# Two plain tiles of an up-projection as one sequence in a fixed order

## The chip, the core and the metric

The kernel runs on one core of a Trainium2 chip. The metric is device time in microseconds (us) of one execution of the whole program; lower is better. TensorE (PE) does the matrix products, VectorE (DVE), ScalarE (ACT) and GpSimd (POOL) work on tiles, SyncE (SP) issues the DMAs. Each of these engines has a queue of its own, and semaphores order the work between them.

## The reference, cut to what matters

One layer of a hybrid backbone: a mixer sub-layer, then a gated MLP with a 3x3 depthwise convolution on the token grid. There are 1024 tokens, 1024 channels, 2816 hidden channels (22 tiles of 128). The change lies where the MLP begins:

```
x   = x + mx[2] * ox                       # ox ends in the product with w_out
hx2 = modulate(rmsnorm(x, norm_ffn_w), mx[3], mx[4])
u, v = split(hx2 @ w_up, 2)                # 22 tiles of u, 22 tiles of v
u   = dwconv2d(u, conv_w, conv_b, 16, 64)  # 9 taps
h   = gelu(u) * v
x   = x + mx[5] * (h @ w_down)
```

Everything is float32. A float32 product is made of three products of a rounded part ("hi") and a remainder ("lo"): hi*hi, hi*lo, lo*hi. So each weight tile and each activation tile is split once: ACT writes hi (a copy to the rounded type), then DVE or POOL writes lo = x - hi.

## The kernel before

**Stages.** After the mixer, `wout` (L1108) makes the w_out product twice, once for each half of the tokens (512 each), 8 tiles of 24 matmuls each time, and adds the result to the residual tiles M0 to M7. Beside the second half, `norm` (L1093) normalizes the first half of the tokens, so that the eight blocks of the first half ("11" and "12", four each, in tiles A0 to A7) are ready when `wout` ends. The second half is normalized only when `wout` has ended, and that runs beside the first two tiles of the up-projection.

**Norm of a half.** `norm` adds up squares over partitions with matmuls against ones (L199), makes 1/sqrt of it in a chain of seven small operations (L182 to L188), spreads it over partitions with matmuls against a scaled identity (L208, L209), and then calls `apply1` for k = 0 to 7: DVE multiplies (a SCALAR_TENSOR_TENSOR, L157), ACT writes the hi half (h), ACT adds the shift in place (q), DVE writes the remainder l = q - h (TENSOR_TENSOR, L160). Blocks k = 0 to 3 are "t12", k = 4 to 7 are "s4"; they stand in tiles H0 to H3 and H8 to H11, and q in H12 to H15.

**Plain tiles.** `up_plain` (L1135) makes hidden tiles f = 0 and f = 1 in the plain way: u and v, for two halves of the tokens, 24 matmuls for each of the eight products (here u0, v0, u1, v1, each with "h0" and "h1" for the halves). u goes to a PSUM tile of pool psD (name d, 2 buffers), v to two of pool psS (name s, 4 buffers). When u is complete, `conv2d` (L1159) lets ACT write bias and middle tap (facc<-d,vec), and DVE adds eight taps (facc<-d,vec,facc); then ACT makes the GELU, DVE multiplies with v, and a DMA stores the tile.

**Strassen tiles.** From f = 2 on, `ups` (L1268) makes each tile with seven products ("11", "12", "s2", "s1", "s3", "s4", "22") of 12 matmuls. They need sums of the activation blocks: `blocks` (L1423) makes "s2", "s1" and "s3" for k = 0 to 3 from the normalized halves, mostly on POOL, and `blocks_late` makes "22" on DVE. In each k, POOL writes t1 (ssq<-H,A), DVE t2 = b22 - t1 (ssq<-H,ssq), ACT and DVE the two parts of t2, POOL t3 (sql<-H), and ACT and POOL the parts of t1 and t3. Product "s2" may begin when ACT has copied "11" out of PSUM (sql<-d), "s1" when DVE has added "12" (d<-d,sql) and ACT has copied "s2" (ssq<-d); these are the waits that `after` (L1250) sets.

**Order.** Up to `ups` a scheduler orders the instructions: `weave` mixes generators, and the scheduler moves instructions that are ready earlier ahead, on each engine apart. `ups` sets `self.pinned`, and from there what goes through `pin` (L1128) stays in the order in which the program writes it. Weights go through `wload` (L78): one DMA to a room raw (2 buffers), then the split into whi0/wlo0 or whi1/wlo1, in turn.

Of the kernel before, what the change touches and what calls it, by code (L numbers as in the profile page):

```python
# [45 lines left out]
class Builder:  # L46
# [129 lines left out]
    def rsqrt(self, pool, ps, n, inv, tag):  # L176

        nc = self.nc
        v = self.t(pool, n, tag + "v")
        a = self.t(pool, n, tag + "a")  # L180
        r = self.t(pool, n, tag + "r")
        nc.vector.tensor_scalar(v, ps, inv, EPS, op0=ALU.mult, op1=ALU.add)  # L182
        self.act(a, v, AF.Sqrt)
        nc.vector.reciprocal(r, a)
        self.tt(a, r, r)
        self.tt(a, a, v)
        nc.vector.tensor_scalar(a, a, -0.5, 1.5, op0=ALU.mult, op1=ALU.add)
        self.tt(r, r, a)  # L188
        return r

    def token_rs(self, pool, parts, n, inv, tag, ps=None):
# [9 lines left out]
        return self.rsqrt(pool, ps[:, :nch], nch, inv, tag)

    def spread(self, pool, r, out, tag):

# [930 lines left out]
    def up_plain(self, f, x, split):  # L1135

        pu = self.t(self.psD, T, "d")
        pv = [self.t(self.psS, H, "s") for _ in range(2)]
        wu = self.wload(self.A["wup"][f])
        wv = self.wload(self.A["wup"][NF + f]) if split else None  # L1140
        for n, hf in ((0, 0), (1, 0), (0, 1), (1, 1)) if split else ((0, 0), (0, 1), (1, 0), (1, 1)):
            if n and wv is None:
                wv = self.wload(self.A["wup"][NF + f])
            blocks = lambda: [x["b"][q][k] for q in (("11", "12"), ("t12", "s4"))[hf] for k in range(4)]
            while any(q is None for q in blocks()):
                next(x["blocks"])
            xh, xl = zip(*blocks())
            yield from self.gdense(pv[hf] if n else pu[:, hf * H : hf * H + H], wv if n else wu, xh, xl, [(0, H)])
            if (n, hf) == (0, 1):
                for _ in self.conv2d(f, pu):  # L1150
                    pass
                acc = self.convacc
        self.act(acc, acc, AF.Gelu_apprx_tanh)
        for i in range(2):
            self.tt(acc[:, i * H : i * H + H], acc[:, i * H : i * H + H], pv[i])
        self.st.dma_start(self.h_d[f], acc)
        yield
# [418 lines left out]
```

## Time and profile before

| | us |
|---|---|
| median of 3 runs | 2314.39 |
| lowest and highest of the runs | 2313.72, 2317.71 |
| profiled execution, its own time | 2316.08 |
| its span, first to last instruction | 2314.3 |
| PE busy in it | 2238.8 (97%) |
| plain tiles, from the first matmul to the first of the Strassen tiles | 1599.34 to 1651.68 |

The profiled execution is 1.69 us above the median, and 1.8 us of it lie outside its span. All places below are in us from the start of the span. A mean granted clock of 0.986 belongs to this execution; 1.00 is the full 2.4 GHz of TensorE, 0.50 is 1.2 GHz.

### The profile page before, as it was taken

What the parts mean: (1) busy time and instruction counts of PE and PEld (TensorE: products, weight loads), DVE (VectorE), ACT (ScalarE), POOL (GpSimd) and SP (SyncE); (2) the same over time, 40 slices, a digit from 0 to 9 for tenths busy, and PEclk for the clock granted to TensorE, in tenths of its full rate; (3) what the DMA queues carried; (4) which work ended last, traced back from release to release, by engine and by line L of the source; (5) the groups of instructions that cost most, each with busy time, mean ns of one, the idle gap of its engine ahead of it and who ended that gap; (6) DMA issues with size and microseconds to landing.
All of it is one profiled execution on the core that took longest, in us unless ns stands there. A gap on an engine that the chain in (4) does not pass through costs nothing.

```text
span 2314.3 us, 29745 instructions
## 1 busy us (share of the span) xinstructions
PE 2238.8 (97%) x11290; PEld 1852.4 (80%) x11290; DVE 1640.5 (71%) x2617; ACT 1150.1 (50%) x1781; POOL 330.0 (14%) x254
## 2 busy tenths in 40 slices
PE   6999999999999999999999999999889999999998
PEld 3778878778888888888888878888668888878888
DVE  4887877789978858767875675547877777774335
ACT  4577667667666647646635332334434444442121
POOL 0000000000000000000000000000757777740000
PEclk7999999999999999999999999999999999999999
DMA  6322322145335333524427775542022222244212
GB/s 250 96 69 73 95 83 65 62 126 159 122 107 172 114 121 106 159 85 130 155 90 267 234 231 191 171 139 73 28 73 82 83 82 82 80 161 129 77 55 73
DMA packets 87795, 274.88 MB, mean 119 GB/s; under 512 B 10434, under 2 KB 16610, under 8 KB 82404
## 3 DMA queue, kind: packets, MB, share of 16 engines
q1 hardware_dynamic: 87648, 272.97, 36.9%
q8 instruction: 89, 1.46, 0.3%
q14 instruction: 54, 0.44, 0.1%
q10 hardware_dynamic: 4, 0.01, 0.0%
HBM read 233.86 MB, written 39.08 MB: 118 GB/s over the span
## 4 chain that ended last, share of the span: by engine, by line
PE 76%; DVE 13%; DMA 5%; ACT 3%; issue 2%; POOL 1%; SPq 0%; POOLq 0%; DVEq 0%; ACTq 0%
PE d L125 30%; PE s L125 18%; PE d L1220 11%; PE s L1220 5%; PE s L986 2%; DMA adar<-in_ada 2%; PE s L651 2%; ACT L L163 1%; DVE wlo L160 1%; PE s L978 1%; DVE L L160 1%; DMA gk<-gd 1%; PE s L927 1%; PE s L926 1%; DVE facc L157 1%
## 5 line engine op out<-in xcount | busy, mean ns | idle before, releaser
L125 PE MATMUL d<-H,whi 128*128 128x512 f32 x2496 | 700.8, 398 | 1.8 <-DVE H L160 1.0
L125 PEld LDWEIGHTS d<-H,whi 128*128 128x128 f32 x2496 | 457.0, 188 | 97.1 <-issue 6.0
L125 PE MATMUL d<-H,wlo 128*128 128x512 f32 x1248 | 392.8, 393 | 1.8 <-DVE wlo L160 1.8
L163 ACT ACTIVATE whi<-raw 128x1024 fp32r<-128x1024 f32 (+2 forms) x194 | 185.7, 959 | 270.7 <-PE s L125 115.4
L125 PEld LDWEIGHTS d<-H,wlo 128*128 128x128 f32 x1248 | 232.9, 188 | 51.6 <-DVE wlo L160 3.5
L157 DVE SCALAR_TENSOR_TENSOR facc<-d,vec,facc 128x945 f32<-128x945 f32 (+2 forms) x176 | 214.6, 1221 | 72.9 <-ACT facc L163 68.6
L160 DVE TENSOR_TENSOR wlo<-raw,whi 128x1024 fp32r<-128x1024 f32 (+1 forms) x154 | 187.5, 1220 | 81.2 <-ACT whi L163 74.4
L125 PE MATMUL s<-H,whi 128*128 128x512 f32 x672 | 202.6, 390 | 1.9 <-ACT whi L163 1.9
L163 ACT ACT_TABLE_LOAD x102 | 130.9, 1283 | 85.9 <-DVE cacc L157 28.7
L1133 POOL TENSOR_TENSOR ssq<-H,A 128x512 f32<-128x512 f32 x4 | 6.0, 1493 | 1162.8 <-ACT H L163 1158.6
L125 PEld LDWEIGHTS s<-H,whi 128*128 128x128 f32 x672 | 125.8, 188 | 29.2 <-ACT whi L163 2.8
L125 PE MATMUL s<-A,whi 128*128 128x512 f32 x480 | 138.2, 390 | 1.0 <-POOL A L1133 1.0
L157 DVE SCALAR_TENSOR_TENSOR M<-s,mods,M 128x512 f32<-128x512 f32 (+1 forms) x72 | 49.5, 690 | 120.4 <-PE s L125 120.3
L125 PE MATMUL s<-H,wlo 128*128 128x512 f32 x336 | 126.0, 391 | 2.1 <-DVE wlo L160 2.0
L125 PEld LDWEIGHTS s<-A,whi 128*128 128x128 f32 x480 | 90.1, 188 | 20.1 <-POOL A L1133 1.4
L157 DVE SCALAR_TENSOR_TENSOR E<-E,cst 128x128 f32<-128x128 f32 x256 | 81.3, 344 | 20.5 <-ACT E L163 20.5
L163 ACT ACTIVATE m<-GU,dtt 128x128 f32<-128x128 f32 x256 | 78.7, 389 | 34.5 <-PE s L978 29.3
L157 DVE SCALAR_TENSOR_TENSOR m<-GL,dtt,m 128x128 f32<-128x128 f32 x256 | 77.7, 346 | 20.3 <-ACT m L163 20.1
L1220 PE MATMUL d<-A,whi 128*128 128x512 f32 x372 | 91.3, 395 | 0.0
L1220 PE MATMUL d<-A,wlo 128*128 128x512 f32 x348 | 85.9, 397 | 5.2 <-ACT ssq L163 5.2
L163 ACT ACTIVATE E<-E,cst 128x128 f32<-128x128 f32 x256 | 80.4, 389 | 17.5 <-DMA E<-csd 17.4
L125 PE MATMUL s<-A,wlo 128*128 128x512 f32 x240 | 83.1, 390 | 0.8 <-DVE wlo L160 0.8
(337 smaller groups left out, 4288.2 us busy)
## 6 DMA issues: line engine op xcount, KB each, us to landing
raw<-in_w SPq DMA_DIRECT2D x92, 512.0 KB, 3.6
E<-csd SPq DMA_DIRECT2D x32, 1024.0 KB, 7.1
A<-in_wup SPq DMA_DIRECT2D x40, 512.0 KB, 4.1
R<-csd SPq DMA_DIRECT2D x64, 256.0 KB, 4.7
adar<-in_ada SPq DMA_DIRECT2D x32, 512.0 KB, 4.0
hd<-facc SPq DMA_DIRECT2D x22, 512.0 KB, 5.1
gated<-sg SPq DMA_DIRECT2D x32, 256.0 KB, 3.8
gd<-y SPq DMA_DIRECT2D x32, 256.0 KB, 2.4
```

The costliest lines, as they stand in the source:

```text
L125: nc.tensor.matmul(o, a[:, k, :], b[k][:, xo + s : xo + e], start=(k == 0 and i == 0), stop=(k == kn - 1 and i == 2))
L157: self.pin(self.nc.vector.scalar_tensor_tensor(out, in0, s, in1, op0=op0, op1=op1))
L160: return self.pin(self.nc.vector.tensor_tensor(out, a, b, op=op))
L163: return self.pin(self.nc.scalar.activation(out, in_, f, **kw))
L651: nc.tensor.matmul(pg, a[:, q, :], b[:, s:e], start=(i == 0), stop=(i == 2))
L926: nc.tensor.matmul(ps[:, s - s2, 0, :], btok[:, s, :], xw[:, 0, s, :], start=True, stop=True)
L927: nc.tensor.matmul(ps[:, s - s2, 1, :], btok[:, 7 - s, :], xw[:, 1, 7 - s, :], start=True, stop=True)
L978: nc.tensor.matmul(psy[q, c, :], self.xt[:, c0 + c, q], m[:, h, c, :], start=True, stop=True)
L986: nc.tensor.matmul(pso[:, c, :], S[:, cc if d == 0 else 7 - cc, d, :], CT[:, cc * P : (cc + 1) * P], start=True, stop=True)
L1133: self.pin(self.nc.gpsimd.tensor_tensor(out, a, b, op=op))
L1220: q = self.pin(self.nc.tensor.matmul(ps, a[:, k, :], b, start=(k == 0 and i == 0 and p in ("11", "12", "s3")), stop=(k == 3 and i == 2), s ...
```

## The change

`up_plain` is replaced by `plain`, which writes both tiles out as one sequence of 64 steps (i = 0 to 63, three matmuls each) and sets `self.pinned` from its beginning. The eight products stand in the order u0 h0, v0 h0, u1 h0, u0 h1, v0 h1, u1 h1, v1 h1, v1 h0. At fixed steps it draws the next piece of the norm, of `blocks` ("sums"), of the two convolutions, and it loads and splits the weights of the first two Strassen products (their splits stood at the head of `ups`). The norm's small operations are pinned too, its PSUM rooms come from pool psS, and its waits are 3 and 4 steps where they were 5 and 3. The weights of u1 go to tiles A14 and A15; the raw weights of f = 3, which had these rooms, are loaded later. `self.wslot = 1` gives u0 the rooms whi0/wlo0 and v0 the rooms whi1/wlo1.

```diff
-        r = self.token_rs(p1, parts, n, 1.0 / D, "fr", self.t(self.psD, T, "d"))
+        room = lambda: self.t(self.psD, T, "d") if pool is None else self.t(pool, H, "s")
+        r = self.token_rs(p1, parts, n, 1.0 / D, "fr", room())
...
+    def plain(self, x, norm, sums):
+        C, b = self.CLASSIC, x["b"]
+        self.wslot = 1
+        w = {"u0": self.wload(self.A["wup"][0]), "v0": self.wload(self.A["wup"][NF])}
+        self.pinned = True
...
+        i = -1
+        for name, f, hf in (("u", 0, 0), ("v", 0, 0), ("u", 1, 0), ("u", 0, 1), ("v", 0, 1), ("u", 1, 1), ("v", 1, 1), ("v", 1, 0)):
...
+            for k in range(8):
+                i += 1
+                if i < 18:
+                    next(norm, None)
+                elif i % 2 == 0:
+                    next(sums, None)
+                for c in (0, 1):
+                    if i == 32 + 16 * c:
+                        conv[c] = [None, self.conv2d(c, pu[c])]
+                    if i in range(32 + 16 * c, 40 + 16 * c, 2):
+                        next(conv[c][1], None)
+                        conv[c][0] = conv[c][0] or self.convacc
+                    if i == 41 + 22 * c:
+                        next(conv[c][1], None)
+                        self.act(conv[c][0], conv[c][0], AF.Gelu_apprx_tanh)
+                if i == 33:
+                    w["v1"] = self.wload(self.A["wup"][NF + 1])
+                if i == 45:
+                    gate(0)
...
+                if i == 56:
+                    self.pslot = 1
+                    for p in ("11", "12"):
+                        self.up_split(C, p, x)
+                p = (("11", "12"), ("t12", "s4"))[hf][k // 4]
+                while b[p][k % 4] is None:
+                    next(norm)
+                bh, bl = b[p][k % 4]
+                for j, (m, n) in enumerate(((hi, bh), (hi, bl), (lo, bh))):
+                    self.pin(self.nc.tensor.matmul(ps, m[:, k, :], n, start=(k == 0 and j == 0), stop=(k == 7 and j == 2)))
+        for _ in sums:
+            pass
+        gate(1)
...
-            x["blocks"] = self.chain(self.norm(sums[1], H, apply1, self.WAIT), blocks())
-            self.weave(self.chain(*[self.up_plain(f, x, f == 0) for f in range(C)]), x["blocks"], self.RATIO[4])
+            for i in range(2):
+                self.up_load(C, i, x)
+            self.plain(x, self.norm(sums[1], H, apply1, (3, 4), self.psS), blocks())
```

**On DVE, the norm of the second half.** M are the residual tiles of k = 0, 1, ...; each H<-M is the multiplication of `apply1`, each H<-H,H the remainder l of a block. Before:

```order
L157 SCALAR_TENSOR_TENSOR H_1823_13111<-M_1685_12373,sc_7_81,d_13095 128x512
L157 SCALAR_TENSOR_TENSOR H_1825_13120<-M_1686_12374,sc_7_81,d_13095 128x512
L157 SCALAR_TENSOR_TENSOR H_1827_13129<-M_1687_12375,sc_7_81,d_13095 128x512
L157 SCALAR_TENSOR_TENSOR H_1829_13138<-M_1688_12376,sc_7_81,d_13095 128x512
L160 TENSOR_TENSOR H_1824_13113<-H_1823_13111,H_1824_13113 128x512
```

and after the change:

```order
L157 SCALAR_TENSOR_TENSOR H_1823_13106<-M_1685_12373,sc_7_81,s_13089 128x512
L160 TENSOR_TENSOR H_1824_13108<-H_1823_13106,H_1824_13108 128x512
L157 SCALAR_TENSOR_TENSOR H_1825_13115<-M_1686_12374,sc_7_81,s_13089 128x512
L160 TENSOR_TENSOR H_1826_13117<-H_1825_13115,H_1826_13117 128x512
L157 SCALAR_TENSOR_TENSOR H_1827_13124<-M_1687_12375,sc_7_81,s_13089 128x512
```

Four multiplications stood ahead of the first remainder; now each remainder stands right behind its own multiplication.

**On ACT, from the blocks' parts to the first copies of the Strassen tiles.** H and A<-ssq and <-sql are parts of the blocks, whi<-raw 128x1024 is the split of a weight tile of v1, facc<-d is the beginning of a convolution, facc<-facc a GELU, sql<-d the copy of product "11". Before (the two splits of 128x1024 are the weights of u1 and of v1):

```order
L163 ACTIVATE A_1845_13212<-ssq_13200 128x512
L163 ACTIVATE whi_1864_13300<-raw_13298 128x1024
L163 ACTIVATE H_1844_13205<-ssq_13201 128x512
L163 ACTIVATE H_1846_13218<-sql_13202 128x512
L163 ACTIVATE A_1851_13236<-ssq_13224 128x512
L163 ACTIVATE whi_1868_13364<-raw_13362 128x1024
L163 ACTIVATE facc_13239<-d_13034,vec_72 128x1024
L163 ACTIVATE H_1850_13229<-ssq_13225 128x512
```

and in the changed kernel, from the parts of k = 2 on:

```order
L163 ACTIVATE H_1851_13252<-ssq_13248 128x512
L163 ACTIVATE A_1853_13263<-ssq_13247 128x512
L163 ACTIVATE facc_13266<-d_13048,vec_72 128x1024
L163 ACTIVATE whi_1856_13275<-raw_13273 128x1024
L163 ACTIVATE H_1858_13282<-sql_13249 128x512
```

The beginning of the first convolution and the split of v1 stand behind the part H<-ssq of k = 2, which waits for DVE's t2 of k = 2; before, they stood ahead of it.

**On ACT, the GELU of tile 1 and the copy of "11".** facc_13352 and facc_13353 are the accumulators of tile 1; whi_1871 and wlo_1872 split the weights of "11" and "12". Before:

```order
L163 ACTIVATE facc_13352<-d_13295,vec_72 128x1024
L163 ACTIVATE wlo_1872_13426<-A_1801_13026 128x512
L163 ACT_TABLE_LOAD
L163 ACTIVATE facc_13239<-facc_13239 128x1024
L163 ACTIVATE whi_1873_13429<-raw_13420 128x512
L163 ACTIVATE wlo_1874_13433<-raw_13420 128x512
L163 ACTIVATE sql_13450<-d_13437 128x512
L163 ACTIVATE whi_1878_13454<-raw_13420 128x512
L163 ACTIVATE facc_13352<-facc_13352 128x1024
```

and after the change:

```order
L163 ACT_TABLE_LOAD
L163 ACTIVATE facc_13266<-facc_13266 128x1024
L163 ACTIVATE facc_13353<-d_13174,vec_72 128x1024
L163 ACTIVATE whi_1871_13395<-A_1801_13026 128x512
L163 ACTIVATE wlo_1872_13398<-A_1801_13026 128x512
L163 ACTIVATE facc_13353<-facc_13353 128x1024
L163 ACTIVATE whi_1873_13429<-raw_13377 128x512
L163 ACTIVATE wlo_1874_13433<-raw_13377 128x512
L163 ACTIVATE sql_13450<-d_13437 128x512
```

The second convolution begins behind the first GELU, and the copy of "11" stands behind the second GELU; before, it was the other way round in both.

## Rows read from the trace of the kernel before

**Rows 1.** Stretches: length, busy us of each engine, granted clock, DMA share, GB/s.

```profile
1599.30:1651.70 52.40, 49.05 (x218) 39.46 (x216) 41.20 (x49) 23.81 (x37) 30.22 (x20) 0.97 0.04 11
1651.70:1670.00 18.30, 13.10 (x48) 10.36 (x48) 16.38 (x15) 7.42 (x11) 12.16 (x9) 0.82 0.23 87
1670.00:1690.00 20.00, 16.75 (x71) 12.83 (x70) 18.45 (x16) 7.66 (x13) 11.82 (x8) 1.00 0.18 52
1690.00:1710.00 20.00, 14.90 (x53) 11.72 (x54) 10.82 (x13) 5.82 (x9) 9.27 (x7) 0.74 0.18 54
1710.00:1730.00 20.00, 20.00 (x90) 16.57 (x89) 14.34 (x15) 9.00 (x14) 14.60 (x12) 1.00 0.26 79
```

**Rows 2.** Timeline of PE: start, us, line, what; in brackets idle time and releaser.

```profile
1599.34 0.61 PE L125 MATMUL d<-A,whi 128*128 128x512 f32 x2
...
1603.42 0.28 PE L199 MATMUL d<-ones,ssq 128*128 128x1 f32 x2
...
1617.94 0.50 PE L125 MATMUL d<-H,whi 128*128 128x512 f32 x1 [1.01 <-DVE H L160]
...
1628.62 0.50 PE L125 MATMUL d<-A,wlo 128*128 128x512 f32 x1 [2.21 <-DVE wlo L160]
...
1651.68 2.95 PE L1220 MATMUL d<-A,whi 128*128 128x512 f32 x12
...
1665.27 5.23 PE L1220 MATMUL d<-A,wlo 128*128 128x512 f32 x12 [5.20 <-ACT ssq L163]
```

**Rows 3.** Timeline of ACT: hi splits of the first two up-projection weights.

```profile
1593.87 1.06 ACT L163 ACTIVATE whi<-raw 128x1024 fp32r<-128x1024 f32 x1 [3.73 <-PE s L125]
...
1599.31 1.06 ACT L163 ACTIVATE whi<-raw 128x1024 fp32r<-128x1024 f32 x1 [3.73 <-PE s L125]
```

**Rows 4.** Timeline of DVE: a weight's lo split, and the second half's norm.

```profile
1600.93 1.22 DVE L160 TENSOR_TENSOR wlo<-raw,whi 128x1024 fp32r<-128x1024 f32 x1
...
1608.81 2.72 DVE L157 SCALAR_TENSOR_TENSOR H<-M,sc,d 128x512 f32<-128x512 f32 x4 [0.58 <-PE d L209]
...
1618.41 0.74 DVE L157 SCALAR_TENSOR_TENSOR H<-M,sc,d 128x512 f32<-128x512 f32 x1
...
1621.48 0.68 DVE L160 TENSOR_TENSOR H<-H,H 128x512 fp32r<-128x512 f32 x1
```

**Rows 5.** Timeline of ACT: the hi half of the norm's last block.

```profile
1619.18 0.73 ACT L163 ACTIVATE H<-H,mods 128x512 fp32r<-128x512 f32 x1 [0.76 <-DVE H L157]
```

**Rows 6.** Timelines of POOL and DVE: operations of the blocks, beside each other.

```profile
1624.52 1.28 POOL L1133 TENSOR_TENSOR H<-sql,H 128x512 fp32r<-128x512 f32 x1
...
1624.59 1.76 DVE L160 TENSOR_TENSOR ssq<-H,ssq 128x512 f32<-128x512 f32 x1 [2.43 <-POOL A L1133]
...
1627.44 2.26 POOL L1133 TENSOR_TENSOR sql<-H 128x512 f32<-128x512 f32 x1
```

**Rows 7.** Timeline of DVE: taps of the two convolutions, addition of "12".

```profile
1635.34 1.21 DVE L157 SCALAR_TENSOR_TENSOR facc<-d,vec,facc 128x960 f32<-128x960 f32 x1
...
1644.23 9.64 DVE L157 SCALAR_TENSOR_TENSOR facc<-d,vec,facc 128x945 f32<-128x945 f32 x8
...
1655.17 6.28 DVE L157 SCALAR_TENSOR_TENSOR facc<-d,vec,facc 128x945 f32<-128x945 f32 x5
...
1663.83 0.69 DVE L160 TENSOR_TENSOR d<-d,sql 128x512 f32<-128x512 f32 x1
```

**Rows 8.** Timeline of ACT: convolution 0's beginning, table load, first GELU, copies of "11" and "s2".

```profile
1632.90 1.19 ACT L163 ACTIVATE facc<-d,vec 128x1024 f32<-128x1024 f32 x1
...
1651.58 1.28 ACT L163 ACT_TABLE_LOAD   x1 [3.31 <-DVE facc L157]
1652.87 1.06 ACT L163 ACTIVATE facc<-facc 128x1024 f32<-128x1024 f32 x1
...
1654.88 0.58 ACT L163 ACTIVATE sql<-d 128x512 f32<-128x512 f32 x1
...
1664.62 0.60 ACT L163 ACTIVATE ssq<-d 128x512 f32<-128x512 f32 x1 [1.50 <-DVE d L160]
```

More of the change, by code (lines that the diff above doesn't have):

```diff
@@ L181, in rsqrt @@
         r = self.t(pool, n, tag + "r")
-        nc.vector.tensor_scalar(v, ps, inv, EPS, op0=ALU.mult, op1=ALU.add)
+        self.pin(nc.vector.tensor_scalar(v, ps, inv, EPS, op0=ALU.mult, op1=ALU.add))
         self.act(a, v, AF.Sqrt)
-        nc.vector.reciprocal(r, a)
+        self.pin(nc.vector.reciprocal(r, a))
         self.tt(a, r, r)
         self.tt(a, a, v)
-        nc.vector.tensor_scalar(a, a, -0.5, 1.5, op0=ALU.mult, op1=ALU.add)
+        self.pin(nc.vector.tensor_scalar(a, a, -0.5, 1.5, op0=ALU.mult, op1=ALU.add))
         self.tt(r, r, a)
@@ L198, in token_rs @@
             for i, q in enumerate(parts):
-                nc.tensor.matmul(ps[:, c : c + 1], q[:, c * P : (c + 1) * P], self.ones[:, 0:1],
-                                 start=(i == 0), stop=(i == len(parts) - 1))
+                self.pin(nc.tensor.matmul(ps[:, c : c + 1], q[:, c * P : (c + 1) * P], self.ones[:, 0:1],
+                                          start=(i == 0), stop=(i == len(parts) - 1)))
         return self.rsqrt(pool, ps[:, :nch], nch, inv, tag)
@@ L207, in spread @@
             dg = self.t(pool, P, tag + "dg")
-            nc.vector.tensor_scalar(dg, self.ident, r[:, c : c + 1], None, op0=ALU.mult)
-            nc.tensor.matmul(out[:, c * P : (c + 1) * P], self.ones, dg, start=True, stop=True)
+            self.pin(nc.vector.tensor_scalar(dg, self.ident, r[:, c : c + 1], None, op0=ALU.mult))
+            self.pin(nc.tensor.matmul(out[:, c * P : (c + 1) * P], self.ones, dg, start=True, stop=True))
     def log1p01(self, e, d, s, q):
@@ L1091, in sumsq, with norm @@
             return sq
-    def norm(self, parts, n, apply, wait):
+    def norm(self, parts, n, apply, wait, pool=None):
         p1, p2 = self.p1, self.p2
@@ L1097, in norm @@
             yield
-        r = self.token_rs(p1, parts, n, 1.0 / D, "fr", self.t(self.psD, T, "d"))
+        room = lambda: self.t(self.psD, T, "d") if pool is None else self.t(pool, H, "s")
+        r = self.token_rs(p1, parts, n, 1.0 / D, "fr", room())
         for _ in range(wait[1]):
             yield
-        ps = self.t(self.psD, T, "d")[:, :n]
+        ps = room()[:, :n]
         self.spread(p2, r, ps, "fr")
@@ L1133, in ptt @@
         self.pin(self.nc.gpsimd.tensor_tensor(out, a, b, op=op))
[L1135 to L1157, printed above, removed]
@@ L1276, in ups @@
         seq += [(None, None)] * (n + 2)
-        self.pslot = 1
         side, free = [], []
-        for i in range(2):
-            self.up_sum(C, i, x)
-        for q in seq[:n]:
+        for q in seq[2:n]:
             self.up_split(*q, x)
```

26 lines of the change are left out of this document (23 added, 3 removed).

## The prediction, made before the changed kernel ran

> **What bounds the kernel now.** The page's busy times come first: PE has far the most of them, so time is lost or won only where PE stands still or runs at the lower clock. Next read the table of stretches [rows 1]: from 1710 on PE is busy 20.00 of 20 us at a granted clock of 1.00, while from 1599 to 1710 it misses 3.35, 5.20, 3.25 and 5.10 us (length minus busy), 16.9 us in all, with the clock at 0.97, 0.82 and 0.74 in three of the four stretches. That is where the change lies, and all that it could win. Since PE has no free time behind 1710, a delay or a gain there goes straight into the end. Then PE's timeline [rows 2] says who makes it wait: the norm's remainders on DVE (1.01 us at 1617.94), a weight's lo part on DVE (2.21 us at 1628.62), and, most of all, ACT's copy of "s2" (5.20 us at 1665.27). That copy comes 0.10 us after DVE's addition of "12" at 1663.83 is over, and DVE is there at the end of a nearly closed run of work: the sixteen taps of the two convolutions, from 1635.34 to 1661.45 [rows 7, 8]. So behind the norm DVE, with ACT and POOL feeding it, sets the pace, not PE. The question of this change is whether the sixteen taps end earlier or later.
>
> **The change part by part.** I go by the profiled execution (2316.08 us; the median of the runs is 1.69 less) and place the changed work on its clock.
>
> *Weights' room of u0.* Before, u0 was split at 1593.87 and v0 at 1599.31, each when `wout`'s products left the room [rows 3]. Now u0 has the room of the last `wout` tile, so it takes the later place: its hi part is there at 1600.4, its lo part (behind two short DVE operations, as the second split stood) at 1600.93 + 1.22 = 1602.15 [rows 4]. The third matmul of u0 starts then; before, it started two matmuls after 1599.34, at 1599.8. PE is 2.4 us late here.
>
> *Order of the products.* 72 instead of 48 matmuls need only the first half. One matmul is 0.227 us (18 matmuls from 1599.34 to 1603.42 [rows 2]), so the 24 more give the norm 5.4 us of cover.
>
> *The norm.* Sums begin after 9 matmuls instead of 18, at 1602.2 + 7 x 0.227 = 1603.8, 0.4 later than before. Sums, root and spreading took 1603.42 to 1608.81 [rows 2, 4]; pinned, with 12 matmuls between sums and spreading, the same path gives about 1609.5. Then the eight blocks. Before, four multiplications ran ahead (2.72 us [rows 4]) and DVE, ACT worked beside each other: 1608.81 to 1622.16, 13.35 us for eight. Now each remainder stands right behind its multiplication, and the next multiplication behind the remainder: 0.77 (multiplication, 0.74, and start of ACT, from 1618.41 to 1619.18 [rows 4, 5]) + 0.76 (h: 0.73 and a hand-over of 0.03) + 0.74 (q, the like) + 0.60 (remainder: 0.68, the next starting 0.08 before its end as in the row of four) = 2.87 us per block. The last block is complete at 1609.5 + 7 x 2.87 + 2.95 = 1632.5, 10.4 us later than before. PE comes to the second half at 1602.2 + 69 x 0.227 + 1.7 (sums) + 1 (spreading) = 1620.6, would need block 7 at 1625.4, and leaves u0 at 1633.0 instead of 1626.0: the cover of 5.4 us is smaller than what the serial norm takes.
>
> *The blocks of "s1", "s2", "s3".* POOL made them from 1621 on, k beside k, as the scheduler found them. Now POOL's order is t1, t3, part of t1, part of t3 for k = 0, then k = 1, and so on, and t2 of k = 0 stands on DVE behind the whole norm. At 1632.5: t2 0.68, ACT's two hi parts to 1634.4, POOL's two lo parts at 1.28 each, so t1 of k = 1 begins at 1636.9. From there a round of k is t1 1.28 + t2 1.76 (DVE beside POOL) + 1.20 (ACT's two hi parts, 0.52 to the second's start, 0.62, two hand-overs of 0.03) + 2 x 1.28 (POOL's lo parts) = 6.8 us. The 1.28 and the 1.76 stand in [rows 6]: DVE's t2 at 1624.59 began beside a POOL operation that ended at 1625.80, and was over 0.55 later, where a remainder of the same size alone took 0.68 [rows 4]; it stood still until POOL was done. The Trainium skill, "SBUF — State Buffer", section "SBUF: two separate sides", has this as a rule: a DVE operation with two SBUF inputs and a GpSimd operation hold a shared port in turn, and the later one waits for all of the other. By that rule t2, which begins just behind the start of t3, takes the 1.76 in every round; with 0.68 each, three rounds would be 3.2 us shorter and the forecast 2.2 us lower, as two of them stand ahead of the first tap.
>
> *The first convolution and v1.* ACT's start of convolution 0 and the split of v1 stand behind the hi parts of k = 2. t1 of k = 2 begins at 1643.7, t2 ends at 1646.8, the hi parts let ACT go at 1647.9: before it was 1632.90 [rows 8]. DVE's first tap is at 1649.1 instead of 1635.34 [rows 7], 13.8 us later. v1's hi part is there at 1650.1, its lo part (behind two taps) at about 1653. PE, which is through u0, v0 and u1 at 1633.0 + 48 x 0.227 = 1643.9, waits 6.2 and 2.3 us and leaves the plain tiles at 1653 + 46 x 0.227 = 1663.5 (before 1651.68).
>
> *From the taps to "s1".* Convolution 0: 8 taps at 1.23 (eight at 9.64 + start, [rows 7]) = 9.8, v1's lo part 1.6, t2 and lo part of k = 3 with their wait 2.1: it ends at 1662.6. Before, the taps of convolution 1 ran under the first GELU. Now ACT makes that GELU first (table load 1.28, GELU 1.06 [rows 8]) and begins convolution 1 behind it (1.19): first tap at 1666.0, last ends at 1675.8 (before 1661.45). Then the second GELU 1.06, two splits 1.04 and only then the copy of "11", before at 1654.88 [rows 8], now at 1677.9; DVE's addition of "12" starts at 1678.5 instead of 1663.83, 14.7 late. Between it and the copy of "s2" stand two more splits which wait for POOL's sums, four POOL operations of 1.3 to 1.8 each: the copy at 1685.0, "s1" at 1685.6 instead of 1665.27, 20 us late. What follows up to 1710 is the same work in the same order; DVE, whose last blocks PE then waits for, is 14.7 late where PE is 20, so a little is made up, and I take 19 us when PE has all it needs. Behind that nothing gives any of it back [rows 1].
>
> *Edits that cost nothing.* The raw weights of f = 3 are loaded later; they are wanted about 15 us after they land now. Their early loads fell in a stretch in which PE never stood still, so leaving them out there wins nothing. Pins on the norm's small operations outside this stretch change nothing, since `pinned` is off there.
>
> Sum: +19 us, 2316.08 + 19 = 2335 for a profiled execution, 2333 for the median. The bounds of what the rows don't show: the round of a block lies between 5.0 us (POOL's four operations at 1.25, everything else beside them) and 8.5 (two of POOL's operations at the 2.26 that [rows 6] show in a collision, 1.0 more each, less what overlaps), so two rounds give -3.6 to +3.4; the lower clock costs nothing more, as PE waits anyway, or 0.2 us (12 matmuls in 5.1 us instead of 2.7 behind 1665.27 [rows 2]) in each of some 40 matmuls of v1 and "11", +8. I take 6.8 and nothing, the values nearest to the rows.
>
> **The rivals.**
> - *The cover wins (faster).* If the second half's parts come in time, PE's stops at 1617.94 and 1628.62 go with the lost clock (1.01 + 2.21 + 0.03 x 52.4), u0 is complete at 1626.0, the taps start and end some 6 us earlier, and the 5.20 go too, less 2.4 for u0: 2314.4 - 10.0 + 2.4 = 2307. It decides from the point where the first tap stands at 1630 or earlier and DVE keeps up behind it. Against it: both orders are fixed in the program, and each engine takes its queue in order; 13.35 us for eight blocks came from an order that is gone.
> - *Only the copy behind the GELU (a little slower).* If the rounds of POOL don't hold ACT, convolution 0 starts at 1634.7 when u0 is complete, and v1 is in time; the taps end at 1661.4, PE leaves at 1653, and the splits and sums before "s1" cost some 5 us: 2319. For it: POOL stood still for 22 of the 52 us before [rows 1]. Against it: t2 of k = 0 needs the end of the norm.
> - *The low clock on top (slower still).* With five stops of 2 to 6 us, PE's clock, at 0.82 and 0.74 in the stretches that held such stops before [rows 1], is low for most of v1 and the first Strassen products, and none of it is covered: 2333 + 8 = 2341.
> - *A delay that is absorbed (no change).* PE would need idle time behind 1710; there is none [rows 1].
>
> The Trainium skill, "PSUM — Partial Sum Buffer", section "Engine vs sequencer instructions", states that the queues of ScalarE, VectorE and GpSimdE are strictly first in, first out. No row here shows one operation passing another on them; if one could pass another that waits, the first rival would hold.
>
> **How the numbers follow.** Forecast 2333 (its own range 2326 to 2338): 0.70. A little slower, 2319: 0.12. Low clock on top, 2341: 0.10. Faster, 2307: 0.04. No change: 0.04. The range 2324 to 2341 holds the forecast, the lower half of the third rival and what lies between the second rival and the forecast. Within 0.2% (4.6 us) of before a measurement of this kernel can't tell a change: 2309.8 to 2319.0. Slower 0.91 (part of the second rival lies inside the bound), same 0.06, faster 0.03.
>
> **What would show it.** In the changed kernel's profile: the norm's eight multiplications on DVE about 2.9 us apart; POOL's t1 of k = 1, 2, 3 about 7 us apart; ACT's start of convolution 0 near 1648; PE waits for ACT's and DVE's parts of v1's weights, then for the copy of "11" before "s2" and for that of "s2" before "s1"; PE without a stop only from about 1723. The prediction is wrong if the first tap stands before 1642, or if "s1" starts before 1675.

## The result, and the profile after

The change made the kernel slower: 2336.73 us (median of 5 runs, 2334.89 to 2337.42) against 2317.71 us of the kernel before (5 runs, 2313.72 to 2320.95), a ratio of 1.0085 (95% interval 1.0073 to 1.0096). The profiled execution took 2335.31 us with a span of 2333.6, 19.3 more than the span before; the forecast was +19.

The stretches of the changed kernel, as in [rows 1] (length, busy us of each engine, granted clock, DMA share, GB/s):

```profile
1599.30:1651.70 52.40, 42.55 (x170) 31.87 (x170) 24.87 (x39) 20.16 (x30) 15.94 (x12) 0.90 0.04 10
1651.70:1670.00 18.30, 16.36 (x58) 12.68 (x59) 14.89 (x15) 6.15 (x8) 11.22 (x9) 0.81 0.17 57
1670.00:1690.00 20.00, 12.32 (x39) 9.24 (x38) 16.12 (x14) 5.25 (x9) 11.46 (x8) 0.74 0.22 80
1690.00:1710.00 20.00, 16.24 (x69) 12.44 (x68) 16.40 (x15) 7.39 (x12) 13.43 (x10) 0.99 0.17 52
1710.00:1730.00 20.00, 15.40 (x56) 12.17 (x57) 10.98 (x13) 6.50 (x10) 9.34 (x7) 0.75 0.19 54
```

PE missed 16.9 us (length minus busy) up to 1710 before; now it misses 9.85, 1.94, 7.68 and 3.76, in all 23.2, and the last stretch, which had no gap, misses 4.6 more and runs at 0.75. DVE shows most plainly that work was put off and not added: in the first stretch it is busy 24.87 us instead of 41.20, over the whole span 1635.9 instead of 1640.5. Over the whole span PE is busy 2246.4 us instead of 2238.8 for the same 11290 matmuls, at a mean granted clock of 0.984 instead of 0.986: of the 19.3 us, 7.6 stand in PE's longer busy time and 11.7 in its waiting.

PE's timeline, as in [rows 2] (start, us, line, what; in brackets idle time and releaser):

```profile
1599.64 0.73 PE L1197 MATMUL d<-A,whi 128*128 128x512 f32 x2 [0.92 <-ACT whi L163]
1601.42 0.50 PE L1197 MATMUL d<-A,wlo 128*128 128x512 f32 x1 [1.05 <-DVE wlo L160]
...
1632.55 0.79 PE L1197 MATMUL d<-H,whi 128*128 128x512 f32 x1 [0.69 <-DVE H L160]
...
1650.03 0.73 PE L1197 MATMUL s<-H,whi 128*128 128x512 f32 x2 [3.32 <-ACT whi L163]
1652.98 0.79 PE L1197 MATMUL s<-H,wlo 128*128 128x512 f32 x1 [2.21 <-DVE wlo L160]
...
1667.67 2.56 PE L1263 MATMUL d<-A,whi 128*128 128x512 f32 x10 [0.63 <-POOL whi L1134]
...
1678.62 4.75 PE L1263 MATMUL d<-H,whi 128*128 128x512 f32 x12 [5.67 <-ACT sql L163]
1685.37 4.62 PE L1263 MATMUL d<-A,wlo 128*128 128x512 f32 x12 [2.00 <-ACT ssq L163]
...
1715.39 1.22 PE L1263 MATMUL s<-H,wlo 128*128 128x512 f32 x2 [2.09 <-DVE H L160]
```

The two stops at the head are u0 in its later room. The stop of 0.69 us at 1632.55 is the last of seven for the norm's blocks. Then come v1's hi and lo parts, the last ten matmuls of "11" (1667.67), the copy of "11" ahead of "s2" (1678.62), and the copy of "s2" ahead of "s1": 1685.37, where [rows 2] had 1665.27. The last row is PE's last stop in these stretches; its like in the kernel before, on the same view:

```profile
1695.89 1.22 PE L1220 MATMUL s<-H,wlo 128*128 128x512 f32 x2 [2.09 <-DVE H L160]
```

It comes 19.5 us later now, and behind it nothing gives that back: from 1730 to 1900 PE is busy 170.00 of 170.00 us in both kernels.

DVE of the changed kernel, as in [rows 4, 6, 7]:

```profile
1609.23 0.75 DVE L157 SCALAR_TENSOR_TENSOR H<-M,sc,s 128x512 f32<-128x512 f32 x1 [0.58 <-PE s L209]
1611.53 0.69 DVE L160 TENSOR_TENSOR H<-H,H 128x512 fp32r<-128x512 f32 x1 [1.55 <-ACT H L163]
1612.14 0.74 DVE L157 SCALAR_TENSOR_TENSOR H<-M,sc,s 128x512 f32<-128x512 f32 x1
...
1631.80 0.69 DVE L160 TENSOR_TENSOR H<-H,H 128x512 fp32r<-128x512 f32 x1 [1.54 <-ACT H L163]
1632.41 0.69 DVE L160 TENSOR_TENSOR ssq<-H,ssq 128x512 f32<-128x512 f32 x1
...
1638.14 1.77 DVE L160 TENSOR_TENSOR ssq<-H,ssq 128x512 f32<-128x512 f32 x1 [3.65 <-POOL ssq L1134]
...
1649.06 2.47 DVE L157 SCALAR_TENSOR_TENSOR facc<-d,vec,facc 128x960 f32<-128x960 f32 x2 [0.92 <-ACT facc L163]
...
1678.60 0.70 DVE L160 TENSOR_TENSOR d<-d,sql 128x512 f32<-128x512 f32 x1 [0.23 <-ACT sql L163]
```

One block of the norm is multiplication, 1.55 us of waiting for ACT, remainder: 2.91 us from 1609.23 to 1612.14, and so on for eight blocks. [Rows 4] had four multiplications in 2.72 us without a wait. The t2 at 1632.41, alone, takes 0.69 us; the one at 1638.14, which begins 0.08 behind a POOL operation, takes 1.77.

POOL's timeline: t1 of k = 1, 2, 3, t3 of k = 1, and the lo part of t3 of k = 2 (1650.57):

```profile
1636.83 1.28 POOL L1134 TENSOR_TENSOR ssq<-H,A 128x512 f32<-128x512 f32 x1
...
1638.06 1.29 POOL L1134 TENSOR_TENSOR sql<-H 128x512 f32<-128x512 f32 x1
...
1643.67 1.29 POOL L1134 TENSOR_TENSOR ssq<-H,A 128x512 f32<-128x512 f32 x1
...
1650.57 1.26 POOL L1134 TENSOR_TENSOR H<-sql,H 128x512 fp32r<-128x512 f32 x1 [1.30 <-ACT H L163]
1651.79 2.26 POOL L1134 TENSOR_TENSOR ssq<-H,A 128x512 f32<-128x512 f32 x1
```

From t1 to t1 it is 6.84 us, then 8.12. The t3 at 1638.06 is the operation that held DVE's t2. And ACT, as in [rows 8]:

```profile
1647.84 1.19 ACT L163 ACTIVATE facc<-d,vec 128x1024 f32<-128x1024 f32 x1
1648.93 1.04 ACT L163 ACTIVATE whi<-raw 128x1024 fp32r<-128x1024 f32 x1
...
1663.59 1.06 ACT L163 ACTIVATE facc<-facc 128x1024 f32<-128x1024 f32 x1
1664.55 1.19 ACT L163 ACTIVATE facc<-d,vec 128x1024 f32<-128x1024 f32 x1
...
1675.99 1.06 ACT L163 ACTIVATE facc<-facc 128x1024 f32<-128x1024 f32 x1 [9.21 <-DVE facc L157]
...
1677.99 0.58 ACT L163 ACTIVATE sql<-d 128x512 f32<-128x512 f32 x1
```

Convolution 0 starts (1647.84) and v1 is split behind two rounds of POOL; the first GELU stands ahead of convolution 1, the second ahead of the copy of "11". PE had made "11" by 1670.23 (the end of the row at 1667.67), but ACT copied it only at 1677.99, behind two splits and a GELU that waited 9.21 us for its taps.

### The profile page after: what moved, and what is told of

The parts are those of the page before. It is cut to its first block, busy times and chain, and to the rows that moved or that the text cites. A ratio compares the mean times of both kernels' runs of the same rounds, so it can differ in the third digit from the quotient of the medians.

```text
span 2333.6 us, 29750 instructions
## 1 busy us (share of the span) xinstructions
PE 2246.4 (96%) x11290; PEld 1854.9 (79%) x11290; DVE 1635.9 (70%) x2617; ACT 1150.5 (49%) x1781; POOL 327.6 (14%) x254
## 4 chain that ended last, share of the span: by engine, by line
PE 76%; DVE 12%; DMA 6%; ACT 3%; issue 3%; POOL 0%; POOLq 0%; SPq 0%; DVEq 0%; ACTq 0%
PE d L125 30%; PE s L125 18%; PE d L1263 11%; PE s L1263 4%; DMA adar<-in_ada 3%; PE s L986 2%; PE s L651 2%; DVE wlo L160 2%; PE s L978 1%; DVE L L160 1%; DVE facc L157 1%; DMA gk<-gd 1%; PE s L927 1%; PE s L926 1%; ACT L L163 1%
## 5 line engine op out<-in xcount | busy, mean ns | idle before, releaser
L125 PE MATMUL d<-H,whi 128*128 128x512 f32 x2464 | 689.8, 398 | 0.7 <-ACT whi L163 0.6
L125 PEld LDWEIGHTS d<-H,whi 128*128 128x128 f32 x2464 | 450.8, 188 | 93.7 <-issue 6.0
L125 PE MATMUL d<-H,wlo 128*128 128x512 f32 x1232 | 386.5, 393 | 2.2 <-DVE wlo L160 2.2
L125 PE MATMUL s<-H,whi 128*128 128x512 f32 x640 | 192.6, 390 | 1.1 <-ACT whi L163 1.1
L125 PEld LDWEIGHTS s<-H,whi 128*128 128x128 f32 x640 | 119.7, 188 | 27.0 <-ACT whi L163 2.0
L125 PE MATMUL s<-A,whi 128*128 128x512 f32 x448 | 128.3, 390 | 1.2 <-POOL A L1134 1.0
L125 PE MATMUL s<-H,wlo 128*128 128x512 f32 x320 | 119.7, 391 | 2.4 <-DVE wlo L160 2.4
L125 PEld LDWEIGHTS s<-A,whi 128*128 128x128 f32 x448 | 83.9, 188 | 19.8 <-POOL A L1134 1.4
L1263 PEld LDWEIGHTS d<-A,whi 128*128 128x128 f32 x372 | 71.0, 191 | 16.5 <-POOL whi L1134 1.1
```

The source lines that it names most:

```text
L125: nc.tensor.matmul(o, a[:, k, :], b[k][:, xo + s : xo + e], start=(k == 0 and i == 0), stop=(k == kn - 1 and i == 2))
L1263: q = self.pin(self.nc.tensor.matmul(ps, a[:, k, :], b, start=(k == 0 and i == 0 and p in ("11", "12", "s3")), stop=(k == 3 and i == 2), s ...
```

## The experiments

All are edits of the changed kernel but e9. The theory: the order in which DVE, ACT and POOL's work is written costs the 19 us, in three links one behind the other (the norm, the rounds with convolution 0 and v1 behind them, the GELUs), and what PE does meanwhile doesn't matter. The rivals: the new list of products, u0's room, or one link alone. Gains are differences of two ratios to the kernel before, times 2316 us; each is uncertain by 3 to 5 us (the two intervals together), so that the traces have to bear them out. A table at the end of this section does that.

**e1_free: the pins taken away.**

```
         w = {"u0": self.wload(self.A["wup"][0]), "v0": self.wload(self.A["wup"][NF])}
-        self.pinned = True
```

> The changed kernel with the same list of products, rooms and early loads, but without the pins from the plain tiles to the Strassen tiles: the scheduler orders them again. Theory (the written order alone costs the 19 us): DVE's multiplications of the norm run ahead again, so the last remainder is over by about 1622 instead of 1632.5, the blocks on POOL are no longer made in step with ACT's queue, the first tap stands at 1636 to 1641 instead of 1649.1 and 's1' starts near 1666 instead of 1685.4: 2317 us, between 2312 and 2322, so no change against the kernel before. Rival 1 (the new list of products or the later room of u0 costs it): 2.4 us for u0 at the least and up to all 19, so 2330 to 2337. Rival 2 (the cover is worth something once it is not spoiled): below 2312.

Measured: 2315.60 us, ratio 1.0000 (0.9990 to 1.0009). The same list of products (PE makes them in that order; only two matmuls of u1 move ahead into u0), the same rooms, the same early loads, and nothing is lost. DVE of this kernel:

```profile
1608.49 2.72 DVE L157 SCALAR_TENSOR_TENSOR H<-M,sc,s 128x512 f32<-128x512 f32 x4 [0.58 <-PE s L209]
...
1620.51 0.68 DVE L160 TENSOR_TENSOR H<-H,H 128x512 fp32r<-128x512 f32 x1
```

and PE at "s1":

```profile
1664.56 4.62 PE L1262 MATMUL d<-A,wlo 128*128 128x512 f32 x12 [4.59 <-ACT ssq L163]
```

Four multiplications run ahead again, and the last remainder is over at 1621.19 instead of 1632.49. "s1" starts at 1664.56. This excludes rival 1 as the cause of the 19 us, and rival 2: the cover wins nothing.

**e6_old_list: the pins kept, the old list of products.**

```
-        for name, f, hf in (("u", 0, 0), ("v", 0, 0), ("u", 1, 0), ("u", 0, 1), ("v", 0, 1), ("u", 1, 1), ("v", 1, 1), ("v", 1, 0)):
+        for name, f, hf in (("u", 0, 0), ("v", 0, 0), ("u", 0, 1), ("v", 0, 1), ("u", 1, 0), ("u", 1, 1), ("v", 1, 0), ("v", 1, 1)):
```

> The changed kernel with the products in the old order (u0 h0, v0 h0, u0 h1, v0 h1, u1 h0, u1 h1, v1 h0, v1 h1) and everything else as it is, pins included. Theory (the written order of DVE, ACT and POOL sets the time, and what PE does meanwhile is worth nothing): PE waits 5.4 us more inside u0 h1 and v0 h1 for the blocks of the norm, and 5.4 us less ahead of v1, whose hi part is there at 1650 in both: 2336 us (2335 to 2338). Rival 1 (the 24 matmuls of cover are worth their 5.4 us): 2340 to 2342. Rival 2 (the new list of products is the cause): 2317 to 2325.

Measured: 2335.85 us, ratio 1.0091 (1.0077 to 1.0105), the same as the changed kernel. PE of this kernel:

```profile
1634.39 0.80 PE L1197 MATMUL d<-H,whi 128*128 128x512 f32 x1 [0.68 <-DVE H L160]
...
1654.85 0.50 PE L1197 MATMUL s<-A,wlo 128*128 128x512 f32 x1 [0.70 <-DVE wlo L160]
...
1668.20 0.73 PE L1263 MATMUL d<-A,whi 128*128 128x512 f32 x2 [2.62 <-ACT whi L163]
...
1687.24 4.49 PE L1263 MATMUL d<-A,wlo 128*128 128x512 f32 x12 [2.28 <-ACT ssq L163]
```

PE waits longer in u0 (eleven stops instead of seven), hardly for v1 (0.70 instead of 3.32 and 2.21), and 2.62 for "11": the wait moves, the end does not. The 5.4 us of cover are worth nothing here, and rivals 1 and 2 fall.

**e2_norm: the multiplication of block k+1 ahead of block k's parts** (`mult1` holds the multiplication that stood in `apply1`).

```
 -            def apply1(k, rs):
+            def mult1(k, rs):
...
                 self.stt(q, x1[k][:, H:], self.sc2[:, k : k + 1], rs, op0=ALU.mult, op1=ALU.mult)
+
+            def apply1(k, rs):
+
+                for j in ((0, 1) if k == 0 else (k + 1,)):
+                    if j < 8:
+                        mult1(j, rs)
+                i = k % 4
+                q = both[i][k // 4]
```

> The changed kernel with one edit: the multiplication of block k+1 is written ahead of ACT's parts and the remainder of block k. Theory (the serial norm is one of three links that add up): a block takes two ACT operations, 1.48 us, instead of 2.90, so the last remainder ends at 1609.2 + 0.8 + 8 x 1.48 + 0.7 = 1622.5 instead of 1632.5; the rounds of the other blocks keep their 6.8 us and everything behind comes 9 to 10 us earlier: ACT's start of convolution 0 at 1638, 's1' near 1676, 2327 us (2325 to 2330). Rival 1 (POOL's rounds are the only link; t1 and t3 of block 0 on POOL wait for the norm's first two operations and not for its end): a gain below 3 us, 2334 to 2337. Rival 2 (the norm is the whole cause): 2317 to 2320.

Measured: 2324.57 us, ratio 1.0039 (1.0024 to 1.0054): 10.7 us gained. DVE of this kernel:

```profile
1612.49 1.41 DVE L157 SCALAR_TENSOR_TENSOR H<-M,sc,s 128x512 f32<-128x512 f32 x2 [0.58 <-PE s L209]
...
1625.36 0.69 DVE L160 TENSOR_TENSOR H<-H,H 128x512 fp32r<-128x512 f32 x1 [0.94 <-ACT H L163]
```

and PE at "s1":

```profile
1678.97 4.61 PE L1263 MATMUL d<-A,wlo 128*128 128x512 f32 x12 [2.16 <-ACT ssq L163]
```

From the first multiplication to the end of the last remainder it is 13.56 us instead of 23.26, 9.7 less (I had expected 13.3). The time lies 0.4 us below my range. A gain below 3 us (rival 1) and a return of the whole (rival 2) fall. (This execution began its norm late, which the last section takes up.)

**e4_gelu: both GELUs written later** (`ups` draws `late` behind product "11" and behind the next).

```
                     if i == 41 + 22 * c:
                         next(conv[c][1], None)
+                    if i == 49 and c == 0:
                         self.act(conv[c][0], conv[c][0], AF.Gelu_apprx_tanh)
-                if i == 45:
+                if i == 57:
                     gate(0)
...
-        gate(1)
+        def late():
+            self.act(conv[1][0], conv[1][0], AF.Gelu_apprx_tanh)
+            yield
+            gate(1)
+            yield
+        x["side"] = [late()]
...
-        side, free = [], []
+        side, free = x.get("side", []), []
...
-            for g in list(side):
+            for g in list(side) if i else []:
```

> The changed kernel with one edit in two places: the first GELU (and its products with v) is written behind the start of convolution 1, the second behind the copy of '11'. Theory: ACT starts convolution 1 at 1657.6, behind the hi parts of k = 3, instead of 1664.6, so that its taps follow those of convolution 0 at 1662 and end at 1672 instead of 1675.9 (the gap on DVE was 1662.2 to 1665.9, less two products of 1.3 us); the copy of '11' comes when PE has made '11' (about 1672.5) instead of behind the second GELU (1678.0), so 's2' starts near 1673 instead of 1678.6, and 's1' near 1678 instead of 1685.4: 2330 us (2327 to 2332). Rival 1 (the taps on DVE hold the sum of '12' anyway): 3.7 us, 2333. Rival 2 (the loss all lies ahead of the first tap): 2336 to 2338.

Measured: 2328.66 us, ratio 1.0055 (1.0039 to 1.0071): 6.9 us gained. ACT of this kernel:

```profile
1660.42 1.19 ACT L163 ACTIVATE facc<-d,vec 128x1024 f32<-128x1024 f32 x1
1665.23 1.28 ACT L163 ACT_TABLE_LOAD   x1 [3.62 <-DVE facc L157]
1666.53 1.06 ACT L163 ACTIVATE facc<-facc 128x1024 f32<-128x1024 f32 x1
...
1672.19 0.60 ACT L163 ACTIVATE sql<-d 128x512 f32<-128x512 f32 x1 [2.10 <-PE d L1270]
```

The norm's first multiplication on DVE, and PE at "s1":

```profile
1612.18 0.75 DVE L157 SCALAR_TENSOR_TENSOR H<-M,sc,s 128x512 f32<-128x512 f32 x1 [0.58 <-PE s L209]
1678.65 3.06 PE L1270 MATMUL d<-A,wlo 128*128 128x512 f32 x12 [1.12 <-ACT ssq L163]
```

Convolution 1 starts ahead of the GELU, and the copy of "11" waits for PE and no longer for ACT's queue. From u0's first matmul to "s1" this trace has 77.63 us (1601.02 to 1678.65) where the changed kernel has 85.73 (1599.64 to 1685.37), although its norm began 1.6 us later behind the last addition of `wout`. Rivals 1 and 2 fall.

**e3_rounds: the blocks of k = 1, 2, 3 behind convolution 0's start and v1.**

```
-                elif i % 2 == 0:
+                elif i % 2 == 0 and not 24 <= i <= 32:
                     next(sums, None)
```

> The changed kernel with one edit: the pieces of the blocks for k = 1, 2, 3 are written behind ACT's start of convolution 0 and behind the load and split of v1. Theory (ACT's queue holds these two behind the hi parts of k = 2): ACT starts convolution 0 at about 1634.7 instead of 1647.8, the first tap stands at 1636, v1 is split by 1639 and PE's two stops of 3.3 and 2.2 us ahead of v1 are gone; but the three rounds of 6.8 us then run beside the taps and end at about 1657, the start of convolution 1 stands behind them and behind the first GELU (1660 instead of 1664.6), and the split of '11', which ACT and POOL make behind the rounds, becomes a new stop of PE. Of 13 us at the first tap some 4 are left at the end: 2333 us (2330 to 2335). Rival 1 (only the norm counts): 2336 to 2338. Rival 2 (the taps' start sets the end): 2324.

Measured: 2331.60 us, ratio 1.0076 (1.0060 to 1.0092): 2.1 us less than the changed kernel, with intervals that overlap. PE of this kernel:

```profile
1669.92 1.22 PE L1263 MATMUL d<-A,whi 128*128 128x512 f32 x2 [5.17 <-ACT whi L163]
1674.55 4.63 PE L1263 MATMUL d<-A,whi 128*128 128x512 f32 x10 [3.41 <-POOL whi L1134]
```

v1's two stops are gone, and PE stands 5.17 and 3.41 us for the parts of "11" in their place. The profiled execution (2339.42 us) is the slowest of the six, 7.8 us above their median; its norm began 15.22 us behind `wout`'s last addition, against 10.48 in the changed kernel. Counted from the norm's first multiplication, the first tap comes 13.1 us sooner than in the changed kernel (26.69 instead of 39.83 us) and "s1" 3.9 us sooner (72.25 instead of 76.14), as the theory had it. So a first tap that comes sooner is worth little while the rounds end as late: rival 2 falls. The times alone can't tell rival 1 from the theory; this trace and e4 speak against it.

**e5_room: u0 in the early room.**

```
-        self.wslot = 1
+        self.wslot = 0
...
-                    self.pslot = 1
+                    self.pslot = 3
```

> The changed kernel with one edit: the weights' rooms in the other turn, so that u0 gets the room that is free 5 us earlier and v0 the room of the last tile of the product with w_out (the first two Strassen splits go to the rooms of v0 accordingly). Theory: PE's two stops of 0.92 and 1.05 us at the head of u0 go, the sums of the norm start about 1.5 to 2 us earlier, and since norm, rounds and taps follow one another, all of it arrives at the end: 2334.5 us (2333 to 2336). Rival 1 (the sums wait for the squares on DVE, not for PE): less than 0.5 us, 2336 to 2337. Rival 2 (v1, which now takes the room of u0 h1's weights, waits longer): slower than 2337.

Measured: 2333.24 us, ratio 1.0078 (1.0066 to 1.0090), 1.6 us better, with overlapping intervals. In the traces the norm's first multiplication stands 7.91 us behind the last addition of `wout` on DVE (1607.19 and 1599.28), 10.48 in the changed kernel (1609.23 and 1598.75): 2.57 us. From there to "s1" the two take the same time (76.11 and 76.14 us). Rival 2 falls, and the trace speaks against rival 1.

**e10_two_links: the edits of e2_norm and e4_gelu together**, as shown above.

> The changed kernel with the edits of e2_norm and e4_gelu together, and nothing else: u0's late room, the rounds of the blocks ahead of convolution 0 and the late splits stay. Theory: norm and GELUs lie one behind the other on the way to 's1', so their gains (10.6 and 6.9 us) add up: 2318.5 us (2316 to 2322), within a few us of the kernel before, with a PE stop of 3.3 and 2.2 us ahead of v1 still there. Rival (with the norm earlier, the GELUs are covered, or the other way round): 2324 to 2326.

Measured: 2316.12 us, ratio 1.0003 (0.9994 to 1.0011): 19.0 us gained, where the two single gains make 17.6. Within what the intervals allow they add up, and the pinned order with two links mended is as fast as the kernel before, though PE still waits for u0 and v1 and the rounds stand where they stood. The rival falls. PE of this kernel:

```profile
1638.71 1.22 PE L1198 MATMUL s<-H,whi 128*128 128x512 f32 x2 [3.26 <-ACT whi L163]
1641.66 0.80 PE L1198 MATMUL s<-H,wlo 128*128 128x512 f32 x1 [1.73 <-DVE wlo L160]
...
1664.39 3.06 PE L1270 MATMUL d<-A,wlo 128*128 128x512 f32 x12 [1.12 <-ACT ssq L163]
```

**e7_all_pinned: the edits of e2, e4 and e5, and the first Strassen splits earlier.**

```
-                if i == 56:
+                if i == 40:
                     self.pslot = 3
```

> The changed kernel, pinned from end to end, with the new list of products, and the written order mended: norm with the multiplications ahead, GELUs behind the start of convolution 1 and behind the copy of '11' (as in the two single edits), u0 in the early room, and the first two Strassen splits written 16 steps earlier, ahead of the rounds for k = 2 and 3. Theory: the single edits measured 10.6 and 6.9 us (differences of their ratios to the kernel before from 1.0085, times 2316), the room about 2, the splits 2 (ACT's and POOL's parts of '11', PE's 0.63); where they overlap some is lost, so 2315 us (2311 to 2319), no longer slower than the kernel before. Rival 1 (a pinned order cannot reach what the scheduler found, because the three links do not add up): 2321 to 2327. Rival 2 (the cover starts to pay): below 2311.

Measured: 2311.39 us, ratio 0.9982 (0.9973 to 0.9990). This order, written out by hand, is a little faster than the scheduler's. Its "s1" starts at 1662.41, with a stop of 0.88 us. Rival 1 falls; whether the cover pays anything here (rival 2) was not tried by itself. Against e10 the norm starts 2.57 us sooner behind `wout`'s last addition (7.91 instead of 10.48) and "s1" stands 1.0 us sooner behind that.

**e8_all_late22 and e9_before_late22: the blocks of "22" begun earlier, in e7 and in the kernel before.**

```
             def blocks_late():
 
-                for _ in range(2):
+                for _ in range(0):
                     yield
```

> The kernel of e7_all_pinned with one more edit: the blocks of '22' are begun two Strassen products earlier. Theory: PE's last stops ahead of the end (1.1, 4.5 and 2.1 us for the blocks of '22', in every kernel so far, the kernel before included) shrink to about 1, while the three subtractions for each block, now ahead of the sum of '12' on DVE, cost 3 to 4 us ahead of 's1': some 4 us less than e7_all_pinned, 2310.5 us (2307 to 2314), below the kernel before. Rival (DVE is full there and only moves its work): 2315, like e7_all_pinned.

> The kernel before with only the one edit that e8_all_late22 has over e7_all_pinned: the blocks of '22' begun two Strassen products earlier. Theory: the edit has nothing to do with the plain tiles and is worth here what it is worth there, or a little more, as PE's last stops (1.1, 4.5 and 2.1 us) stand in the kernel before too, and 3 to 4 us are paid ahead of 's1': 2312 us (2309 to 2315), which lies above e8_all_late22 by what e7_all_pinned is below the kernel before (4 us). Rival (the scheduler's plain tiles leave DVE so full that the three subtractions ahead of the sum of '12' cost all of it): 2316.

Measured: e8 2308.65 us, ratio 0.9969 (0.9957 to 0.9980), the fastest of all; e9 2310.00 us, ratio 0.9976 (0.9966 to 0.9985). PE of e9 around "s1" and "22":

```profile
1665.86 5.49 PE L1220 MATMUL d<-A,wlo 128*128 128x512 f32 x12 [8.62 <-ACT ssq L163]
...
1689.05 0.73 PE L1220 MATMUL s<-H,wlo 128*128 128x512 f32 x2 [0.45 <-DVE H L160]
```

The stops of 4.46 and 2.09 us for the blocks of "22" are gone, and the stop ahead of "s1" grew from 5.20 [rows 2] to 8.62. My expectation that e8 would keep e7's lead of 4 us over e9 was too high: 1.6 us are left, and the intervals overlap. Why the two gains don't add was not tried. What beats the kernel before by the larger part is an edit outside the plain tiles.

**All traces side by side.** Where an execution begins its norm differs by several us, so the links are best read from the norm's first multiplication (DVE) to "s1" (PE), in us of each profiled execution; beside it stands the start of that multiplication behind the start of `wout`'s last addition on DVE.

| kernel | multiplication behind `wout` | from it to "s1" |
|---|---|---|
| before | 9.27 | 56.46 |
| changed | 10.48 | 76.14 |
| e1_free | 9.50 | 56.07 |
| e6_old_list | 11.99 | 76.14 |
| e5_room | 7.91 | 76.11 |
| e3_rounds | 15.22 | 72.25 |
| e2_norm | 15.24 | 66.48 |
| e4_gelu | 12.05 | 66.47 |
| e10_two_links | 10.48 | 56.81 |
| e7_all_pinned | 7.91 | 55.81 |

The change costs 19.7 us in this stretch. The norm returns 9.66 of them, the GELUs 9.67, both together 19.33: they add up, and each is half of the loss. The list of products and u0's room change nothing in it; nor does PE's clock, for PE is busy 5.1 us longer in e6 than in the changed kernel (2251.5 and 2246.4 over the span). The rounds return 3.9 by themselves, yet e10 leaves them and is 0.35 us from the kernel before: of the three links of the theory, two make the loss. One execution of each kernel stands behind these figures.

## Why the prediction was right

**The mechanism** held: the order written out by hand, on engines that take their queues in turn, was worse than what the scheduler had found, and the cover for PE was worth nothing. e1 and e6 show both halves: without pins nothing is lost with the new list, with pins nothing changes with the old one. That the queues go in turn shows on ACT: the copy of "11" waited from 1670.23 to 1677.99 behind a GELU and two splits.

**Step by step.** *u0's room*: the third matmul was forecast 2.61 us behind the start of `wout`'s last addition (1602.15, and 1599.54 in the execution before), measured 2.67 (1601.42 and 1598.75); taking the early room again (e5) starts the norm 2.57 us sooner. *The norm*: 2.87 us per block forecast, 2.90 measured (1609.23 to 1629.51 for seven); last remainder at 1632.5, measured 1632.49; undoing it alone returned 10.7 us, 9.66 by the trace. That places agree to 0.1 us is in part luck: this execution ended `wout` 0.79 us sooner than the one on whose clock I worked, and its norm began 0.52 us later behind that than forecast (10.48 instead of 9.96). *Rounds*: 6.8 forecast, 6.84 for the one between k = 1 and 2, t2 with 1.77 us beside POOL as in [rows 6]. The rule of the shared port that the prediction weighed (the Trainium skill, "SBUF — State Buffer", section "SBUF: two separate sides") agrees with these two t2 (0.69 alone, 1.77 behind a POOL operation). *Convolution 0*: ACT's start 1647.9, measured 1647.84; first tap 1649.1, measured 1649.06. *v1*: waits of 6.2 and 2.3 us, measured 3.32 and 2.21. *Convolution 1*: first tap 1666.0, measured 1665.88. *Copy of "11"* 1677.9, measured 1677.99; *"s1"* 1685.6, measured 1685.37.

**Sizes that were off.** v1's first wait is 2.9 us shorter, since PE came there later: it left u0 at 1633.57 where I had put 1633.0, and the 48 matmuls from there to its stop, which begins at 1646.71, took 13.1 us where I had put 10.9 at full clock. The granted clock was 0.50 from 1628.00 to 1633.30, in u0's stops, and still from 1633.50 to 1637.40. It left the plain tiles at 1666.31 instead of 1663.5 for the like reason (0.50 from 1653.00 to 1658.00). That was time PE had to spare. The round of k = 2 took 8.12 us instead of 6.8: POOL waited 1.30 us for ACT's part of t3 (the row at 1650.57), which stands behind convolution 0's start and v1's hi part. And t1 of k = 3, beside DVE's lo part of v1 (1651.45 to 1652.92), took 2.26. Both lie behind the hi parts that release the first tap, so the terms ahead of that were not touched. "PE without a stop only from about 1723" was wrong: the last stop ends at 1715.39, which is the old 1695.89 plus 19.5; I had worked it out from no row. Of the 1.3 us that I expected to be made up between "s1" and there, 0.6 was (30.62 us before, 30.02 now). And the term "GELUs", which I had spread over two sentences, weighs as much as the norm: 6.9 us by the times, 9.67 by the trace. The 3.4 us that the sum took for the rounds ahead of the first tap stand there (30.16 us from the norm's first multiplication to the first tap in e10, 26.53 before), but e10 shows that they don't reach "s1": there the sixteen taps take 23.09 us from first to last, before 26.11, with DVE waiting in between (2.56 us ahead of t2 at 1640.83).

**The rivals.** "The cover wins" would have needed the first tap at 1630; it stood at 1649.06, and e1, where DVE works as freely as before, gives no gain either. "Only the copy behind the GELU" needed convolution 0 to start at 1634.7; the rounds held ACT until 1647.84, and e4, which takes that copy from behind the GELU, leaves 12.7 us of loss (ratio 1.0055), so this link was not the whole. "The low clock on top": there was more low clock (0.90, 0.81, 0.74 and 0.75 in four stretches, 0.97, 0.82 and 0.74 in three of [rows 1]), and PE was busy 7.6 us longer, but the span grew by 19.3 us, no more than the queues explain, and e6, with more of it, takes the same 76.14 us to "s1".

## What to carry to other kernels

When an order that a scheduler found is replaced by one written out, go through each engine's queue and ask for every instruction that waits what stands behind it: a producer written right behind the consumer of the one before makes a pipeline serial (2.9 us per block, 1.7 in e2), and a GELU that still waits for its taps (9.21 us here) holds the copy written behind it, which another engine needs. Work for the busiest engine that "covers" a wait was worth nothing here, as the engines that set the pace got their own work no sooner. Undo the order alone (e1) and the list alone (e6) first: two runs split the change.

## What the runs showed of the hardware

The head of the plain tiles is the same program in the changed kernel and in e2_norm up to the norm's first multiplication, yet that took 9.59 us from u0's first matmul in one execution (1599.64 to 1609.23) and 14.36 in the other (1598.13 to 1612.49). The stretch up to it, in the changed kernel:

```profile
1599.60:1609.20 9.60, 8.36 (x46) 6.90 (x47) 4.90 (x13) 1.24 (x2) 0.00 (x0) 1.00 0.19 55
```

and in e2_norm:

```profile
1598.10:1612.50 14.40, 13.16 (x46) 10.82 (x47) 4.90 (x14) 1.26 (x2) 0.00 (x0) 0.64 0.13 37
```

The granted clock was 1.00 in the one and 0.64 in the other (0.50, which is 1.2 GHz, from 1602.00 to 1610.00), behind the same two stops of 0.92 and 1.05 us. So a low clock that PE has to spare elsewhere costs 4.8 us where DVE waits for PE's sums, and the profiled execution of e2 (2328.74 us) is the slowest of its six runs (2321.50 at best). The six pinned kernels that have these two stops began the norm 10.48 (twice), 11.99, 12.05, 15.22 and 15.24 us behind the last addition of `wout`. In the three kernels with u0 in the early room that were profiled (e5, e7, e8), where the stops are gone, it was 7.91 us each time; one execution each does not show that this is why.
